# Three branch gates ahead of the mixers' end, halved block transposes and a later second low-rank visit in a hybrid transformer block

## The chip, the cores and the metric

The kernel runs on one core of a Trainium2 chip. TensorE (PE in the profile) multiplies matrices, VectorE (DVE) does elementwise arithmetic and 32x32 block transposes, ScalarE (ACT) does activations and rounding copies, GpSimd (POOL) does a few small operations, and SyncE (SP) issues the weight transfers. The metric is the device time in microseconds of one execution; lower is better. Times given as a median are over repeated runs; a profile shows one execution.

## The reference

One layer works on 256 tokens of 2048 features in fp32:

```
u = RMSNorm_pre(x)
proj = u @ w_in            # attention A (q,k,v), attention B (q,k,v,f), RWKV inputs, three gates
y_A = stick-breaking attention, y_B = forgetting attention, y_C = RWKV-7 time mixing (16 heads x 64)
m = sigmoid(g_a)*(y_A @ w_branch_a) + sigmoid(g_b)*(y_B @ w_branch_b) + sigmoid(g_c)*(y_C @ w_branch_c)
x = x + RMSNorm_post(m @ w_out)
x = x + RMSNorm_post2(relu(RMSNorm_pre2(x) @ w_up)^2 @ w_down)
```

The change lies where y_C is finished and where the third term of m, the one with g_c, begins.

## The kernel before, in words

**Weights.** All weights lie in DRAM as one stream of tiles of 128x1024 fp32 (512 KB), `wst`. `wraw` (L159) issues the next tile's DMA on SP's queue into one of three buffers `raw`; `wsplit` (L169) has ACT round it into `whi` (L172) and DVE subtract that from the tile to give `wlo` (L174). A product in fp32 is then made of three matmuls in the fp32r type: high by high, high by low, low by high. `wnext` (L177) keeps one tile ahead. The order of the tiles is that of the stream, except where the table `jump` (L153) gives another successor. `gc` is the first tile of the third branch. From there the stream holds, for each of four column groups g, eight tiles of gate weights (`gc + 12*g` on) and four tiles of `w_branch_c` (`gc + 12*g + 8` on). So in this kernel the order is: gate 0, gate 1, branch 0, branch 1, gate 2, branch 2, gate 3, branch 3.

**Products.** `unit` (L199) makes 128 output columns out of two tiles. `tok` (L207) makes 512 output columns for both halves of the tokens: for all tiles but the last it issues 12 matmuls (L234) and after that the last tile's 12 in two groups of six (`prod`, L219), one for each half of the tokens. So a gate, with eight tiles, is 84 matmuls of L234 and 12 of L219; a branch, with four tiles, is 36 and 12. `gate` (L999) runs `tok` on the normed input and has ACT write tanh into tiles `th` (L1003); its tiles have either their own tag or the tag `BK`, whose eight buffers the time mixing uses as well. `branch` (L1007) runs `tok` on the mixers' output and has DVE multiply by the gate (L1014) and add into `m` (L1015).

**Two strands of work.** PE's program order is that of the Python code. The products are one strand. The other is a generator, `mixers` (L943): attention A, attention B, the low-rank inputs of RWKV, and then `rwkv_half` (L665) for heads 0-7 and for heads 8-15. The products call `tick` (L137) a few times for each tile (in `tok` 0.7, 0.5 and 0.5, in `unit` 1.0 and 1.0). Each tick adds 0.62 times its argument to `credit` (at most 1.5) and takes its argument from `hold`; when `hold` is not positive and `credit` is, the generator is resumed. What it yields is the step's cost, taken from `credit`; a yield of `("stage", cost, h)` ends the resuming for this tick and sets `hold` to h (2.0 without h). So a pause h delays the generator by h worth of ticks. Order on the other engines is left to the compiler's scheduler; each engine then runs its own instructions in order.

**rwkv_half, in order.** The squares of k and the inverse norms; then for each of four pairs of heads its visit. A visit begins, for the first two pairs, with `gates` (L716) for two pairs at a time, whose low-rank matmuls (L723) take two of the four PSUM buffers `mps`; the visit itself (L771 to L790) takes four `mps` buffers for score blocks (L775), a transpose and a head sum, and DVE (L784, L789) and ACT (L787) read them out. At its end stands L790, `yield ("stage", 1.6)`. After the four visits 32x32 blocks are transposed on DVE into `U` (L814), a triangular system is solved in 31 steps (L819, L821), and the result is transposed back by DVE into `TW` (L825) and `SC` (L829). A scan over four chunks follows (L853 to L905, its last matmuls on `Bt` in L885), and then the group norm and output gate of the half, two pairs of heads at a time (L907 to L941): head sums on PE (L100, L101), gate products (L926, L929), an inverse root on ACT and DVE (`rsqrt`, L262 to L269) and products on DVE (L936 to L939).

**The third branch.** `cut` (L1025) splits each finished pair of heads of y_C into a high and a low part (L255 on ACT, L256 on DVE). L1033 runs two gates, with `cut` called at each tick; L1034 then resumes the generator until it ends, without any tick between; after that the branches run, the last tile of each in need of heads 12 to 15:

```
    thc = [gate(), gate("BK", 8)]
    while not fin[0]:
        step()
    cut()
```

Of the kernel before, what the change touches and what calls it, by code (L numbers as in the profile page):

```python
# [52 lines left out]
def hybrid_block(ctx, tc, xt, x, gains, params, consts, lora, gup, wst, out):  # L53
    nc = tc.nc
    V, A, G, PE = nc.vector, nc.scalar, nc.gpsimd, nc.tensor
# [10 lines left out]
    def nm(s):  # L66
        uid[0] += 1
        return f"{s}_{uid[0]}"
# [4 lines left out]
    def mps():  # L73
        return pm.tile([128, 512], F32, tag="mps", name=nm("mps"), bufs=4)
# [4 lines left out]
    def tmp(n=T):  # L79
        return tpool.tile([128, T], F32, tag="tmp", name=nm("tmp"), bufs=3)  # L80
# [5 lines left out]
    def C(name, r=slice(0, 128), lo=0, hi=None):  # L86
        c0, w = CC[name]
        hi = w if hi is None else hi
        if name == "ident":
            return ident[r, lo:hi]  # L90
        if c0 < NR + 128:
            return cr[r, c0 - 128 + lo:c0 - 128 + hi].bitcast(F32)
        return con[r, c0 - 128 - NR + lo:c0 - 128 - NR + hi]

    def CR(name):
        c0 = CC[name][0] - 128
        return cr[:, c0:c0 + 128]

    def twice(o, w, hi, lo):
        PE.matmul(o, w, hi, start=True, stop=False)  # L100
        PE.matmul(o, w, lo, start=False, stop=True)  # L101
# [48 lines left out]


    gc = wst.shape[0] - 256 - 32 - 48
    jump = {23: 28, 53: 24, 27: 54, gc + 7: gc + 12, gc + 19: gc + 8, gc + 11: gc + 20}  # L153
    wq = []
    side = []

# [50 lines left out]
    def tok(pks, lag=1, mid=()):  # L207


        ps = [gps(), gps()]  # L210
        n = len(pks)
        kept = []

        def prod(hl, k0, tt):
            for w, parts in ((hl[0], (0, T)), (hl[1], (0,))):
                for k in (k0, k0 + 1):
                    for part in parts:
                        c = part + tt * 128
                        PE.matmul(ps[tt], pks[k][:, c:c + 128], w[:, (k - k0) * 512:(k - k0) * 512 + 512],  # L219
                                  start=k == 0 and part == 0 and w is hl[0], stop=w is hl[1] and k == n - 1)  # L220

        for k0 in range(0, n, 2):
            hl = wnext()
            if k0 >= n - 2 * lag:
                prod(hl, k0, 0)
                kept.append((hl, k0))
                tick()
                continue
            for w, parts in ((hl[0], (0, T)), (hl[1], (0,))):
                for k in (k0, k0 + 1):  # L230
                    for tt in range(2):
                        for part in parts:
                            c = part + tt * 128
                            PE.matmul(ps[tt], pks[k][:, c:c + 128], w[:, (k - k0) * 512:(k - k0) * 512 + 512],  # L234
                                      start=k == 0 and part == 0 and w is hl[0], stop=False)
                    if w is hl[1] or k == k0:
                        tick(0.7 if w is hl[0] else 0.5)
        yield ps[0]
        for i, (hl, k0) in enumerate(kept):
            prod(hl, k0, 1)  # L240
            tick()
            if i < len(mid):
                mid[i]()
        yield ps[1]
# [31 lines left out]
    def g1(w=T):  # L276
        return rp.tile([128, T], F32, tag="g1", name=nm("g1"), bufs=21)
# [387 lines left out]
    def rwkv_half(hf):  # L665
# [12 lines left out]
        for i2 in range(2):  # L678
            hi, lo = pair(), pair()
            for i, p in enumerate(PR[2 * i2:2 * i2 + 2]):  # L680
                yield ("need", f"k{p}")
                kx[p] = done[f"k{p}"]
                s = tmp()
# [27 lines left out]
        SC = rp.tile([128, 32, 128], F32, tag="SC", name=nm("SC"), bufs=1)  # L711
# [52 lines left out]
        for i, p in enumerate(PR):  # L764
            for j in ((0, 1), (2, 3), (), ())[i]:
                yield from gates(j, PR[j])
            yield ("need", f"v{p}")
            yield ("stage", 0.4, 2.5 if i == 0 else 0)
            v, kp = done[f"v{p}"], kps[p]

            pss = [mps(), mps()]  # L771
            for cc in range(4):
                for h in range(2):
                    hr = slice(64 * h, 64 * h + 64)
                    PE.matmul(pss[h][:, cc * 128:cc * 128 + 128], At[p][hr, cc, :], Bt[p][hr, cc, :],  # L775
                              start=True, stop=True)
            psk = mps()
            for cc in range(4):
                PE.transpose(psk[:, cc * 128:cc * 128 + 128], At[p][:, cc, :], C("ident"))
            psb = mps()  # L780
            twice(psb[:, 0:T], CR("bones"), kp[:, 0, :], kp[:, 1, :])
            for h in range(2):
                s0 = i * 8 + h * 4
                V.tensor_tensor(SC[:, s0:s0 + 4, :], pss[h].rearrange("p (c t) -> p c t", c=4),  # L784
                                C("scm").unsqueeze(1).to_broadcast([128, 4, 128]), ALU.mult)
            Kt[p] = rp.tile([128, 4, 128], F32, tag="BK", name=nm("Kt"), bufs=8)
            A.activation(Kt[p], psk.rearrange("p (c t) -> p c t", c=4), AF.Copy)  # L787
            bon[p] = g1()
            V.tensor_tensor(bon[p], psb[:, 0:T], v, ALU.mult)  # L789
            yield ("stage", 1.6)  # L790

        pss = [mps(), mps()]
        for i, p in enumerate(PR):
# [12 lines left out]
        U = rp.tile([64, 32, 32], F32, tag="b6", name=nm("U"), bufs=1)  # L806
        Ti = rp.tile([64, 32, 32], F32, tag="Ti", name=nm("Ti"), bufs=1)
# [3 lines left out]
        G.memset(Tf[:, 0:1024:33], 1.0)  # L811
        for b in range(2):
            br = slice(32 * b, 32 * b + 32)
            V.transpose(out=U[br], in_=SC[br, :, 32 * b:32 * b + 32].rearrange("s l t -> s t l"))  # L814
            yield 1.3
        for s in range(31):
            n, m = 31 - s, s + 1
            t3 = tp[:, 0:n * m].rearrange("p (a b) -> p a b", a=n)
# [3 lines left out]
            yield 0.15 + n * m * 2.1e-3  # L822
        TW = rp.tile([64, 32, 32], F32, tag="b6", name=nm("TW"), bufs=1)

        V.transpose(out=TW[0:32].rearrange("t l i -> t i l"), in_=Ti[0:32].rearrange("l t i -> l i t"))  # L825
        yield 1.3
        for b in range(2):
            br = slice(32 * b, 32 * b + 32)
            V.transpose(out=SC[br, :, 32 * b:32 * b + 32].rearrange("i l t -> i t l"), in_=Ti[br])  # L829
            yield ("stage", 1.3, 1 + 3 * b)  # L830

        ps = mps()
        for j in range(32):
# [109 lines left out]
    def mixers():  # L943
        yield from sb_mix()
        yield from fox_mix()
        yield from rwkv_lora()
        for hf in range(2):
            yield from rwkv_half(hf)
# [15 lines left out]
    for br in ("sb", "fox"):  # L964
        for s in ("q", "k"):
# [3 lines left out]
            for h in range(4):  # L969
                ps = unit(upk)  # L970
                t = g1()
# [27 lines left out]
    def gate(tag="th", bufs=3):  # L999
        ths = []  # L1000
        for ps in tok(upk):
            th = rp.tile([128, 512], F32, tag=tag, name=nm("th"), bufs=bufs)
            A.activation(th, ps, AF.Tanh, scale=0.5)  # L1003
            ths.append(th)
        return ths
# [24 lines left out]

    cut()
    each.append(cut)
    thc = [gate(), gate("BK", 8)]  # L1033
    while not fin[0]:  # L1034
        step()
    cut()
# [52 lines left out]
    for c in range(0, D, 512):  # L1089
        for tt in range(2):  # L1090
            loads.append(lambda tt=tt, c=c: nc.sync.dma_start(out=x1[tt][:, c:c + 512],
                                                              in_=x[tt * 128:tt * 128 + 128, c:c + 512]))
# [410 lines left out]
    for g in range(4):  # L1503
        gs = slice(512 * g, 512 * g + 512)
        for tt, ps in enumerate(tok(hp, 4 if g == 3 else 1)):
# [8 lines left out]
            if g == 3:  # L1514
                for c, w in (0, 512), (512, 512), (1024, 512), (1536, 256), (1792, 256):
# [3 lines left out]
                        out=out[tt * 128:tt * 128 + 128, cs], in_=x1[tt][:, cs])  # L1519
# [125 lines left out]
```

## Time and profile before

| | us |
|---|---|
| median of three runs | 1519.75 (1519.08 to 1521.86) |
| the profiled execution | 1519.93 |
| its span, first to last instruction | 1518.2 |
| PE busy | 1495.3 (98%) |
| weight loads on PE busy | 1254.8 (83%) |
| DVE busy | 1208.3 (80%) |
| ACT busy | 939.7 (62%) |
| POOL busy | 99.6 (7%) |

The 1.7 us between the execution and its span lie outside the first and last instruction. The profile numbers time from the span's start. The attention and RWKV inputs, the mixers and the three branches fill about the first 830 us; the output projection and the MLP fill the rest. A row of a timeline gives start, duration, engine, line, operation, output and inputs, shape and count; in brackets stands how long the engine was idle before and what released it. A row of the chain gives start, duration, engine, output and line of a piece of work on the path that ends last.

### The profile page before, as it was taken

The numbers are of one execution on the slowest core, as the hardware profiler recorded it, in microseconds if no ns is written. First come the engines' busy times: TensorE is split into PE (matmuls) and PEld (weight loads), VectorE is DVE, ScalarE is ACT, GpSimd is POOL, SyncE is SP. The second block draws the span as 40 slices with busy tenths as digits, with TensorE's granted clock in tenths as the row PEclk, the third lists the DMA queues.
The fourth block names the chain that finished last, engine by engine and source line by source line (L and its number), as shares of the span: only waits on it lengthen the run. The fifth ranks groups of instructions, "written<-read, shape, count | busy, mean of one in ns | idle before, by whom it ended". The sixth has DMA issues, their size and how long they took to land.

```text
span 1518.2 us, 22692 instructions
## 1 busy us (share of the span) xinstructions
PE 1495.3 (98%) x8384; PEld 1254.8 (83%) x8384; DVE 1208.3 (80%) x1663; ACT 939.7 (62%) x1433; POOL 99.6 (7%) x151
## 2 busy tenths in 40 slices
PE   9999999999999999989999999999999999999997
PEld 7888888887787877778888988888888888888886
DVE  7875669985678885565656778999899989999996
ACT  7665677545776445644445766677666666766663
POOL 0031003000002000000000000000000000000000
PEclk9999999999999999999999999999999999999999
DMA  7645454454455464445575758879888888889874
GB/s 266 194 167 181 148 172 156 157 190 144 157 170 181 145 195 147 156 152 194 203 249 189 242 173 263 235 226 275 247 256 265 242 249 245 263 263 259 253 221 151
DMA packets 104687, 312.71 MB, mean 206 GB/s; under 512 B 10240, under 2 KB 12288, under 8 KB 104576
## 3 DMA queue, kind: packets, MB, share of 16 engines
q1 hardware_dynamic: 93968, 279.87, 55.2%
q0 software_dynamic: 8064, 29.36, 10.1%
q10 hardware_dynamic: 2544, 2.03, 0.5%
q8 instruction: 66, 1.08, 0.3%
q14 instruction: 45, 0.37, 0.1%
HBM read 279.77 MB, written 2.10 MB: 186 GB/s over the span
## 4 chain that ended last, share of the span: by engine, by line
PE 86%; DVE 6%; DMA 3%; issue 2%; ACT 2%; DVEq 0%; POOLq 0%; SPq 0%; POOL 0%; ACTq 0%
PE gps L234 25%; PE gps L190 19%; PE gps L194 11%; PE gps L219 7%; PE mps L1363 3%; PE mps L1365 3%; PE mps L1364 3%; PE gps L1363 2%; PE gps L1365 2%; PE gps L1364 2%; DMA raw<-in_wst_dram 2%; DVE wlo L174 2%; PE gps L196 1%; ACT whi L172 1%; DMA raw<-raw 1%
## 5 line engine op out<-in xcount | busy, mean ns | idle before, releaser
L174 DVE TENSOR_TENSOR wlo<-raw,whi 128x1024 fp32r<-128x1024 f32 x576 | 697.7, 1221 | 176.0 <-ACT whi L172 158.5
L172 ACT ACTIVATE whi<-raw 128x1024 fp32r<-128x1024 f32 x576 | 603.9, 1056 | 257.1 <-PE gps L234 91.7
L190 PE MATMUL gps<-pk,whi 128*128 128x512 f32 x1479 | 375.7, 392 | 1.8 <-DVE tmp L1281 1.6
L190 PEld LDWEIGHTS gps<-pk,whi 128*128 128x128 f32 x1479 | 273.9, 188 | 57.7 <-DVE tmp L1281 2.6
L234 PE MATMUL gps<-whi,pk 128*128 128x512 f32 x1004 | 254.6, 392 | 0.0
L194 PEld LDWEIGHTS gps<-pk,wlo 128*128 128x128 f32 x1582 | 215.5, 190 | 15.7 <-DVE wlo L174 0.8
L194 PE MATMUL gps<-pk,wlo 128*128 128x256 f32 x1582 | 221.1, 282 | 0.0
L234 PEld LDWEIGHTS gps<-whi,pk 128*128 128x128 f32 x1004 | 186.4, 188 | 39.7 <-issue 0.8
L234 PE MATMUL gps<-wlo,pk 128*128 128x512 f32 x502 | 137.7, 392 | 1.1 <-DVE wlo L174 1.1
L234 PEld LDWEIGHTS gps<-wlo,pk 128*128 128x128 f32 x502 | 93.2, 188 | 21.9 <-DVE wlo L174 2.0
L1363 PE MATMUL mps<-whi,fm 128*128 128x512 f32 x224 | 88.6, 396 | 0.8 <-ACT whi L172 0.5
L1364 PE MATMUL mps<-whi,fm 128*128 128x512 f32 x224 | 87.7, 392 | 0.0
L1280 ACT ACTIVATE tmp<-gps 128x256 f32<-128x256 f32 x64 | 24.6, 384 | 101.7 <-PE gps L196 99.8
L1365 PE MATMUL mps<-wlo,fm 128*128 128x512 f32 x224 | 87.4, 390 | 0.0
L1343 POOL DMA_DIRECT2D raw<-raw x56 | 48.8, 872 | 573.2 <-DVE raw L1340 279.8
L1340 DVE TENSOR_TENSOR raw<-raw,raw 128x1024 f32<-128x1024 f32 x56 | 68.3, 1220 | 0.8
L219 PE MATMUL gps<-whi,pk 128*128 128x512 f32 x224 | 63.0, 404 | 4.6 <-ACT pk L255 4.6
L1363 PE MATMUL gps<-whi,fm 128*128 128x512 f32 x168 | 65.8, 392 | 0.0
L1365 PE MATMUL gps<-wlo,fm 128*128 128x512 f32 x168 | 65.8, 392 | 0.0
L1364 PE MATMUL gps<-whi,fm 128*128 128x512 f32 x168 | 65.5, 390 | 0.0
L219 PEld LDWEIGHTS gps<-whi,pk 128*128 128x128 f32 x224 | 42.3, 193 | 14.4 <-ACT pk L255 5.0
L1365 PEld LDWEIGHTS mps<-wlo,fm 128*128 128x128 f32 x224 | 42.1, 188 | 9.6 <-DVE wlo L174 0.2
(346 smaller groups left out, 1732.2 us busy)
## 6 DMA issues: line engine op xcount, KB each, us to landing
raw<-in_wst_dram SPq DMA_DIRECT2D x516, 512.0 KB, 4.4
raw<-raw POOLq DMA_DIRECT2D x56, 512.0 KB, 8.2
x<-in_xt_dram SPq DMA_DIRECT2D x8, 256.0 KB, 6.8
x<-in_x_dram SPq DMA_DIRECT2D x8, 256.0 KB, 5.0
raw<-in_wst_dram SPq DMA_DIRECT2D x4, 256.0 KB, 4.8
g<-in_gains_dram SPq DMA_DIRECT2D x4, 256.0 KB, 4.9
pk<-in_gains_dram SPq DMA_DIRECT2D x4, 256.0 KB, 7.4
out_dram<-x SPq DMA_DIRECT2D x4, 256.0 KB, 2.8
```

Source lines behind the costliest of these rows:

```text
L172: A.activation(hi, raw, AF.Copy)
L174: low = lambda: V.tensor_tensor(lo, raw, hi.bitcast(F32), ALU.subtract)
L190: PE.matmul(ps, hi[:, i * 128:i * 128 + 128], pks[i], start=first and i == 0, stop=False)
L194: PE.matmul(ps[:, 0:T], lo[:, i * 128:i * 128 + 128], pks[i][:, 0:T], start=False, stop=False)
L219: PE.matmul(ps[tt], pks[k][:, c:c + 128], w[:, (k - k0) * 512:(k - k0) * 512 + 512], start=k == 0 and part == 0 and w is hl[0], stop=w is ...
L234: PE.matmul(ps[tt], pks[k][:, c:c + 128], w[:, (k - k0) * 512:(k - k0) * 512 + 512], start=k == 0 and part == 0 and w is hl[0], stop=False)
L1280: A.activation(b, ps[:, T:2 * T], AF.Copy)
L1340: V.tensor_tensor(R[d, a], R[d, a], R[d, b], ALU.add)
L1343: G.dma_start(out=R[d, a], in_=R[d, b], accum_op=ALU.add)
L1363: PE.matmul(Q[f], a, w, start=d == d0 and i == 0, stop=False)
L1364: PE.matmul(Q[f], b, w, start=False, stop=False)
L1365: PE.matmul(Q[f], a, wl, start=False, stop=d == dn and i == 1)
```

## The change

There are four edits.

1. A third gate, for column group 2, is run at L1033 before the generator is driven to its end, with its two output tiles in `BK` buffers.
2. `jump` is rewritten so that the weight tiles come in the new order: gate 0, gate 1, gate 2, branch 0, branch 1, branch 2, gate 3, branch 3.
3. The pause after the visit of the first pair (L790) becomes 3.5 ticks in place of the default 2.0; other pairs keep 2.0.
4. Each of the five block transposes of a half (two of L814, one of L825, two of L829) is made in two instructions of half the columns. Each half has a step cost of 0.65 in place of 1.3 for the whole; the pauses at L830 become 0.5, 0.5, 0.5 and 3.5 in place of 1 and 4.

```diff
-    jump = {23: 28, 53: 24, 27: 54, gc + 7: gc + 12, gc + 19: gc + 8, gc + 11: gc + 20}
+    jump = {23: 28, 53: 24, 27: 54, gc + 7: gc + 12, gc + 19: gc + 24, gc + 31: gc + 8,
+            gc + 11: gc + 20, gc + 23: gc + 32}
...
-            yield ("stage", 1.6)
+            yield ("stage", 1.6, 3.5 if i == 0 else 2.0)
...
-            V.transpose(out=U[br], in_=SC[br, :, 32 * b:32 * b + 32].rearrange("s l t -> s t l"))
-            yield 1.3
+            for c in (slice(0, 16), slice(16, 32)):
+                V.transpose(out=U[br, c], in_=SC[br, :, 32 * b:32 * b + 32][:, :, c].rearrange("s l t -> s t l"))
+                yield 0.65
...
-        V.transpose(out=TW[0:32].rearrange("t l i -> t i l"), in_=Ti[0:32].rearrange("l t i -> l i t"))
-        yield 1.3
+        for c in (slice(0, 16), slice(16, 32)):
+            V.transpose(out=TW[0:32, :, c].rearrange("t l i -> t i l"), in_=Ti[0:32, :, c].rearrange("l t i -> l i t"))
+            yield 0.65
...
-            V.transpose(out=SC[br, :, 32 * b:32 * b + 32].rearrange("i l t -> i t l"), in_=Ti[br])
-            yield ("stage", 1.3, 1 + 3 * b)
+            for c in (slice(0, 16), slice(16, 32)):
+                V.transpose(out=SC[br, :, 32 * b:32 * b + 32][:, :, c].rearrange("i l t -> i t l"), in_=Ti[br, c])
+                yield ("stage", 0.65, 0.5 + 3 * b * (c.start > 0))
...
-    thc = [gate(), gate("BK", 8)]
+    thc = [gate(), gate("BK", 8), gate("BK", 8)]
```

## The prediction, made before the result was known

> **What bounds the kernel now.** The first thing to read is the busy time on the page.
>
> ```profile
> PE 1495.3 (98%) x8384; PEld 1254.8 (83%) x8384; DVE 1208.3 (80%) x1663; ACT 939.7 (62%) x1433; POOL 99.6 (7%) x151
> ```
>
> PE is busy for 98% of the span, and the change takes no matmul away. All that it can win is time in which PE waits or runs slowly. So the second view is that of the waits, for PE alone, over the stretch of the mixers, 220 to 660 us (in total, how often, the longest):
>
> ```profile
> PE gps L219 <- ACT pk L255: 4.6, 1, 4.6
> PE gps L234 <- DVE wlo L174: 1.1, 2, 0.9
> PE gps L219 <- DVE wlo L174: 1.0, 2, 0.6
> PE mps L723 <- DVE SC L784: 0.9, 1, 0.9
> ```
>
> That is everything: 7.6 us in six waits, of which one alone is 4.6. The same view from 662.65 to 860 us names no wait of PE. The chain of waits, third, shows what the long one is:
>
> ```profile
> 642.65 0.23 PE mps L100
> ...
> 657.13 0.42 ACT pk L255
> 657.55 0.04 issue
> 657.60 5.22 PE gps L219 x12
> 662.82 8.16 PE gps L234 x36
> 670.98 2.72 PE gps L219 x12
> 673.70 19.04 PE gps L234 x84
> 692.74 2.72 PE gps L219 x12
> ```
>
> Gate 1 ends at 642.65. The head sums of the last two pairs (L100) come right behind it, and from there a serial tail runs over ACT and DVE: two table loads with the logarithm and exponential, the inverse root, the products, the split (L255). It ends at about 657.6, after 15 us. Beside it PE has only the first three tiles of branch 0 (about 8.2 us by the row of 36 matmuls); the fourth needs the last heads. The 12 matmuls of that fourth tile take 5.22 us where all their like take 2.72. The stretches show why (busy us and count of PE, weight loads, DVE, ACT, POOL, then the granted clock, the DMA's share and GB/s):
>
> ```profile
> 653.00:657.60 4.60, 0.00 (x1) 0.00 (x1) 4.38 (x11) 1.74 (x5) 0.00 (x0) 0.77 0.65 218
> 657.60:660.00 2.40, 2.40 (x6) 1.86 (x7) 0.74 (x2) 0.28 (x1) 0.00 (x0) 0.50 0.45 176
> 660.00:662.65 2.65, 2.65 (x8) 2.12 (x7) 1.38 (x2) 0.30 (x1) 0.00 (x0) 0.56 0.02 6
> 662.65:665.40 2.75, 2.75 (x14) 2.27 (x13) 2.43 (x3) 1.45 (x2) 0.00 (x0) 1.00 0.00 0
> ```
>
> The granted clock falls during the wait and stays at 0.50 to 0.56 until 662.65. So the wait costs 4.6 us and then 5.22 - 2.72 = 2.5 us more, 7.1 in all.
>
> **The third gate.** It puts eight tiles of work that need no mixer between gate 1's end and branch 0: 84 and 12 matmuls, 19.04 + 2.72 = 21.8 us by the last rows of the chain. Does the tail fit under it? By the code, after the head sums the generator still yields 0.1 + 2.2 + 1.1 + 1.1 = 4.5 of cost. A tile of a gate gives 1.7 ticks, 1.05 of credit, so these steps take 4.3 tiles. The pause before the head sums (2.5 ticks) adds at most 1.5 tiles. Edit 3 delays each half by at most a tile of a gate (seven ticks in place of four), less what credit is kept over the pause. At worst the generator ends after 4.3 + 1.5 + 2 = 7.8 of 8 tiles. Behind its last step stand at most some 4.6 us of DVE and ACT (the stretch from 653.00 to 657.60 has all of it, DVE 4.38 busy), and branch 0's fourth tile comes another 8.2 us after the gate. There is room even then. I take the whole **7.1 us** as gained; the bounds are 7.1 and, if the tail still ends last, 0 (below, as a rival).
>
> What the gate brings with it is moved and not new: eight transfers, eight roundings on ACT, eight subtractions on DVE, two tanh. In SP's queue the eight loads go ahead of branches 0 and 1; from 600 to 720 us that queue holds nothing else, and POOL's holds nothing:
>
> ```profile
> raw<-in_wst_dram SPq DMA_DIRECT2D x37, 512.0 KB, 3.2
> ```
>
> The new tanh tiles need two more BK buffers. The last reader of Bt there starts before 620 us, some 40 us before the third gate's first tanh could write, so ACT waits for no buffer:
>
> ```profile
> L885 PE MATMUL mps<-Bt,Pb x96: 222/222/270, 361.6 to 618.7; 128*64 128x64 f32 x96
> ```
>
> Three branches now follow one another where two did. A branch has 8.16 + 2.72 = 10.9 us of PE; DVE's share is four subtractions of 1.2 us and four products and sums of 0.69 (the rows of L174 and L1014 below), 7.6 us. That hides, and two in a row showed no PE wait.
>
> **The pause.** The wait of L723 is for PSUM: its two buffers come free when L784 has read the first pair's scores.
>
> ```profile
> 247.76 0.98 PE L723 MATMUL mps<-xs,lors 64*128 64x256 f32 x12 [0.88 <-DVE SC L784]
> 248.23 0.40 DVE L789 TENSOR_TENSOR g<-mps,g 128x256 f32<-128x256 f32 x1
> ```
>
> In this half the ticks are 1.0, so 3.5 means two ticks or one tile more (about 2.7 us). By then L784 and L789 have ended, and the wait goes: **0.9 us**, bounds 0 and 0.9. The other half's L723 shows no wait and only gets later. Behind the delayed visit stand all later steps of the generator; they end at most two tiles later, which the third gate covers as worked out above. Without that gate it would lengthen the 4.6 us.
>
> **The transposes.** Price of one, and what a short DVE instruction costs (ns least/median/most in the first row):
>
> ```profile
> L814 DVE STREAM_TRANSPOSE U<-SC x4: 2003/2016/2027, 276.7 to 504.1; 32x1024 f32<-32x1024 f32 x4
> ```
> ```profile
> 507.28 0.19 DVE L819 TENSOR_TENSOR tp<-U,Ti 64x31 f32<-64x31 f32 x1
> ...
> 522.36 0.42 DVE L819 TENSOR_TENSOR tp<-U,Ti 64x256 f32<-64x256 f32 x1
> ```
>
> From 31 to 256 elements 0.23 us are added, about 1.0 ns an element, which leaves 0.16 us that doesn't scale. The trace shows no half transpose. If it shrinks with its elements it takes 1.0 us, or 1.1 with 0.16 fixed; if it doesn't shrink at all, 2.0. I take 1.1, the row of the same engine, so ten more instructions add 1.6 us of DVE in two halves. [...]
>
> What the halves give: a subtraction can pass between them. Two of PE's waits lie at transposes:
>
> ```profile
> 329.68 2.06 DVE L829 STREAM_TRANSPOSE SC<-Ti 32x1024 f32<-32x1024 f32 x1
> ...
> 333.44 1.20 PE L234 MATMUL gps<-wlo,pk 128*128 128x512 f32 x4 [0.91 <-DVE wlo L174]
> ```
> ```profile
> 549.00 1.06 ACT L172 ACTIVATE whi<-raw 128x1024 fp32r<-128x1024 f32 x1 [0.92 <-DMA raw<-in_wst_dram]
> ...
> 550.94 0.72 PE L219 MATMUL gps<-wlo,pk 128*128 128x512 f32 x2 [0.56 <-DVE wlo L174]
> ```
>
> The first I believe: the subtraction stood behind this whole transpose and the one before it. The second has a late transfer ahead of it, which only in part goes back to DVE. Bounds 0 and 0.9 + 0.6 = 1.5; I take **0.7**, near the middle.
>
> **New small waits.** Steps of the mixers now meet other tiles. The waits for wlo that lie at no transpose sum to 1.1 + 1.0 - 1.5 = 0.6 us now. They may go (0.6 gained) or as much as all 2.1 us of waits for wlo may come anew. I take 0.6 lost.
>
> **Sum.** 7.1 + 0.9 + 0.7 - 0.6 = 8.1 us. The profiled execution took 1519.93, which gives 1511.8; it lies 0.18 above the median of the runs, so in terms of that median **1511.6 us**. The likeliest case's own range: all gains at their best (7.1 + 0.9 + 1.5 + 0.6 = 10.1) give 1509.6; the gate's gain alone less 2.1 gives 1514.7.
>
> **The rivals.**
>
> *A wait remains under the new gate.* The tail now competes with eight tiles' roundings and subtractions where it had four, and PE waits for some wlo, or for the last split, again. For it: from 642 to 653 us ACT was nearly full (9.2 of 11 us). Against: PE waited for nothing in these 11 us, with the same tail beside it.
>
> ```profile
> 500.00:553.00 53.00, 52.44 (x261) 43.03 (x258) 51.21 (x91) 24.23 (x32) 0.00 (x0) 1.00 0.48 159
> 642.00:653.00 11.00, 10.98 (x49) 8.30 (x47) 6.08 (x8) 9.16 (x11) 0.00 (x0) 1.00 0.38 118
> ```
>
> Price: from where the likeliest range ends to half of the 7.1 and a little, 1514.7 to 1516.7. Chance 0.08. Waits up to 0.9 us left the clock at 1.00 in this trace and the one of 4.6 did not. [...]
>
> *The change doesn't do what it says.* The generator, slowed by two pauses, still ends last, behind the gate, and the wait with its clock comes back whole: 1511.6 + 7.1 = 1518.7, within 0.2% of before. It needs the tail to be over 12 us later than worked out. Chance 0.04.
>
> *Slower: half a transpose costs as much as a whole.* Then each half of the heads gets five more instructions of 2.0 us, 10 us. Place: the stretch from 500 to 553 us and its like in the first half of the heads. DVE is busy there for 51.2 of 53 us, so only 1.8 us hide; the other 8.2 us push the subtractions back and PE with them, twice: 16.4 us, 1528.0. It decides from 1.8 us for a half transpose on, where two times (5 x 0.8) us eat the 8.1. Against it: DVE's other rows shrink with their elements, L819 above, and L1014 with half of L174's elements takes 0.69 to its 1.22 us:
>
> ```profile
> L174 DVE TENSOR_TENSOR wlo<-raw,whi 128x1024 fp32r<-128x1024 f32 x6 | 7.3, 1220 | 4.2 <-ACT whi L172 4.2
> ...
> L1014 DVE SCALAR_TENSOR_TENSOR th<-th,gps 128x512 f32<-128x512 f32 x2 | 1.4, 689 | 3.1 <-PE gps L219 3.1
> ```
>
> Chance 0.06.
>
> **How the numbers follow.** The forecast has 0.82, the rivals 0.08, 0.04 and 0.06. A measurement of this kernel can tell about 0.2% (3.0 us) from no change, so faster means under 1516.7. That holds for the forecast's range and the first rival: 0.82 + 0.08, from which I give 0.03 to "same" since the first rival's end lies on that line. Faster 0.87, same 0.07, slower 0.06. The range goes from 1509.5 to 1516.0: the forecast's own and most of the first rival, leaving the second and third out.
>
> **What would show it.** Right: no wait of PE over 1 us between 600 and 700 us, a granted clock of 1.00 there, the branch's six-matmul groups all near 1.36 us; L723 without a wait in the first half; half transposes near 1.1 us; no wait at the first half's L829. Wrong: a wait on L255 or on wlo in the third gate, half transposes near 2 us, or new waits on wlo between 250 and 600 us that sum to more than 2 us.

## The result and the profile after

The changed kernel took **1511.3 us** (median of eight runs, 1509.64 to 1513.97); the kernel before took 1519.3 in eight runs beside them (1516.52 to 1521.86). The ratio is 0.9953, with a 95% interval of 0.9944 to 0.9962: 5.8 to 8.5 us faster. The profiled execution of the changed kernel took 1513.32 us, 2 us above its median, with a span of 1511.5. Code lines in its profile are one to four higher than before.

First the waits of PE over the mixers, 220 to 660 us, in total, how often and the longest:

```profile
PE gps L235 <- DVE wlo L175: 1.9, 1, 1.9
PE mps L845 <- ACT TW L841: 0.7, 4, 0.2
```

The wait of 4.6 us is gone, and so are the one at the low-rank matmuls (L723 before) and all the old waits for wlo. Two kinds that were not there before stand in their place: one wait of 1.9 us for wlo, and four of up to 0.2 us each at L845. The chain of work around gate 1's end, with start and duration:

```profile
642.38 2.72 PE gps L220 x12
645.10 4.99 PE gps L235 x22
650.08 0.23 PE mps L100
...
652.04 14.28 PE gps L235 x62
666.32 2.72 PE gps L220 x12
669.03 8.16 PE gps L235 x36
677.20 2.72 PE gps L220 x12
```

Only PE stands in it now. The head sums come 5 us into the third gate, the tail runs beside the rest of the gate, and the fourth tile of branch 0 (677.20) takes 2.72 us. The granted clock is 1.00 from 640 to 675 us. The last split, from the timeline:

```profile
663.48 0.75 DVE L257 TENSOR_TENSOR pk<-g,pk 128x256 fp32r<-128x256 f32 x2
```

It ends at 664.2, 13 us before the tile that needs it. But gate 1 ends at 645.10, where it ended at 642.65 before: up to here the changed kernel is 2.4 us behind, with the same work done (4095 instructions of PE in both). Further on it is ahead. The first transpose of the MLP's input, on PE, before and after (the duration in ns, then first and last start in us):

```profile
L1125 PE MATMUL mps<-ident,x x32: 270/272/328, 827.0 to 837.8; 128*128 128x128 f32 x32
```
```profile
L1129 PE MATMUL mps<-ident,x x32: 270/272/328, 822.3 to 833.1; 128*128 128x128 f32 x32
```

It starts 4.7 us earlier, so 2.4 + 4.7 = 7.1 us were won between gate 1's end and 827 us. The last 2.0 us of the 6.7 by which the spans differ come in the MLP, which the change doesn't touch: the profile before has 1.6 us of waits on evictions there (L190) that this one lacks. That part is not steady from one execution to the next. In the thirteen profiles of this case, from the row above to the end of the span, it takes between 688.7 and 691.2 us.

Where the 2.4 us went shows in stretches (busy us and counts of PE, weight loads, DVE, ACT and POOL, then the granted clock, DMA's share and GB/s):

```profile
344.00:346.50 2.50, 1.81 (x66) 1.22 (x66) 1.23 (x1) 2.39 (x5) 0.00 (x0) 1.00 0.48 164
346.50:350.50 4.00, 4.00 (x12) 3.08 (x11) 1.22 (x1) 2.31 (x7) 0.00 (x0) 0.57 0.71 245
468.30:469.60 1.30, 1.30 (x6) 0.85 (x8) 1.30 (x2) 0.42 (x1) 0.00 (x0) 1.00 0.31 63
469.60:473.20 3.60, 3.60 (x24) 3.28 (x25) 2.59 (x5) 1.54 (x2) 0.00 (x0) 0.53 0.88 286
```

Behind each of the two places with new waits lies a stretch of about 3.4 us at a granted clock of 0.50 (the 0.57 and 0.53 above are means that take in its edges), where PE has work. The 12 matmuls of branch 0's last tile took 5.22 us at 0.50 to 0.56 in the kernel before and take 2.72 at 1.00 here; if the work in these stretches also takes about half as long at 1.00, each can cost up to 1.7 us, which is an estimate. New waits of 1.9 + 0.7 and old ones of 0.9 + 2.1 gone leave 0.4 us won, so to be 2.4 us behind, the two stretches must have cost 2.4 + 0.4 = 2.8 us in this one execution. That is a difference, not a measurement of its own, and it fits under the 3.4 us that two such stretches can cost.

### The profile page after: what moved, and what is told of

Same layout as the page of the kernel before. It is cut to its first block, busy times and chain, and to the rows that moved or that the text cites. A ratio compares the mean times of both kernels' runs of the same rounds, so it can differ in the third digit from the quotient of the medians.

```text
span 1511.5 us, 22706 instructions
## 1 busy us (share of the span) xinstructions
PE 1494.9 (99%) x8384; PEld 1256.2 (83%) x8384; DVE 1208.5 (80%) x1673; ACT 938.9 (62%) x1433; POOL 99.5 (7%) x151
## 3 DMA queue, kind: packets, MB, share of 16 engines
q8 instruction: 66, 1.08, 0.3%
## 4 chain that ended last, share of the span: by engine, by line
PE 90%; DVE 4%; DMA 3%; issue 2%; ACT 1%; DVEq 0%; POOLq 0%; SPq 0%; POOL 0%; ACTq 0%
PE gps L235 26%; PE gps L191 21%; PE gps L195 11%; PE gps L220 7%; PE mps L1367 3%; PE mps L1369 3%; PE mps L1368 3%; PE gps L1369 2%; PE gps L1367 2%; PE gps L1368 2%; DMA raw<-in_wst_dram 2%; PE gps L197 1%; DVE wlo L175 1%; DMA raw<-raw 1%; PE mps L776 1%
## 5 line engine op out<-in xcount | busy, mean ns | idle before, releaser
L235 PEld LDWEIGHTS gps<-whi,pk 128*128 128x128 f32 x1004 | 187.0, 188 | 40.1 <-issue 0.8
L1367 PEld LDWEIGHTS mps<-whi,fm 128*128 128x128 f32 x224 | 42.3, 189 | 9.1 <-ACT whi L173 3.0
```

Source lines behind the costliest of these rows:

```text
L1367: PE.matmul(Q[f], a, w, start=d == d0 and i == 0, stop=False)
```

## The experiments

Each kernel is timed against the kernel before on the same chip. The medians of before in the four sets were 1518.44, 1518.1, 1518.33 and 1518.86 us.

### Each edit by itself

**The third gate alone** (edits 1 and 2; the lines of `jump` are those of the change):

```diff
...
-    thc = [gate(), gate("BK", 8)]
+    thc = [gate(), gate("BK", 8), gate("BK", 8)]
```

> The third gate and its tile order alone, pause and transposes as before. My account (the wait of 4.6 us and 2.5 us at half clock both go, because 21.8 us of gate cover the tail): 7.1 us faster, some 1512.3 by the first median, no wait of PE near 650 us, granted clock 1.00 there, and the waits at L723 (0.9) and on wlo (2.1) still there. Rival (the gate gives only the wait, and the rest of the measured 8 us comes from pause and transposes): 4.6 us faster, some 1515.

Measured: 1511.62 us, ratio 0.9960 (0.9948 to 0.9972), so 4.3 to 7.9 us faster; the medians lie 6.8 apart. Its chain:

```profile
639.97 2.72 PE gps L220 x12
642.69 0.23 PE mps L100
...
644.65 19.27 PE gps L235 x84
663.91 2.72 PE gps L220 x12
666.63 8.16 PE gps L235 x36
674.79 2.72 PE gps L220 x12
```

Until gate 1's end nothing has moved (642.69 to 642.65), and its small waits up to there are those of the kernel before. The fourth tile of branch 0 takes 2.72 us, the time of its like in the kernel before at a granted clock of 1.00. The 7.1 us lie within the interval and so do 4.6. The trace decides: from the same gate 1's end, the first transpose of the MLP's input (L1126 here) starts at 819.9 us where it started at 827.0, so 7.1 us are gone and not 4.6.

**The pause alone** (edit 3):

```diff
-            yield ("stage", 1.6)
+            yield ("stage", 1.6, 3.5 if i == 0 else 2.0)
```

> The longer pause alone, with two gates. My account: the 0.9 us wait of L723 goes, but the generator is up to two tiles later at gate 1's end, so more of the tail lies behind it and the wait before branch 0's last tile grows from 4.6 us by 0 to 5 us: same to 4 us slower. Rival (the pause is free, its delay is made up by kept credit): 0.9 us faster, wait unchanged at 4.6.

Measured: 1520.82 us, ratio 1.0013 (1.0005 to 1.0022), 0.8 to 3.3 us slower. Its waits from 220 to 665 us:

```profile
PE mps L100 <- ACT hl L919: 3.2, 1, 3.2
PE gps L234 <- DVE wlo L174: 2.6, 3, 1.9
PE gps L219 <- DVE pk L256: 0.8, 1, 0.8
PE gps L219 <- ACT pk L255: 0.5, 1, 0.5
PE mps L101 <- DVE hl L920: 0.2, 1, 0.2
```

The wait of L723 is gone. In the place of the 4.6 us stand 3.2 + 0.2 at the head sums and 1.3 behind: about as much, but earlier, since the later tail doesn't have its head sums' inputs ready when gate 1 ends. And a wait of 1.9 us for wlo is new. So the pause isn't free, and the delay shows where I expected it, in another form. But all these waits sum to 7.3 us, where those of before sum to 7.6, so they are not what makes the kernel slower. Behind the 1.9 us, the next 34 matmuls of PE take 6.5 us (465.73 to 472.26), where the same 34 take 4.9 with gate and pause (465.85 to 470.80), at a clock of 1.00: 1.6 us more, or by estimate some 3.2 us at half clock. Behind the 3.2 us lie some 6.8 us of it:

```profile
647.00:650.00 3.00, 2.77 (x10) 1.51 (x9) 1.50 (x2) 2.60 (x4) 0.00 (x0) 0.67 0.07 26
650.00:655.00 5.00, 5.00 (x13) 3.73 (x12) 1.39 (x2) 3.30 (x4) 0.00 (x0) 0.51 0.23 89
```

PE has work in nearly all of it. In the kernel before, the slow clock (0.50) also lasts some 6.8 us, but it begins about 2 us before the wait ends, while PE has nothing to do. The cost of the pause alone is that of the clock more than that of waits.

**The halved transposes alone** (edit 4; its diff is that of the change):

> The halved transposes alone, with two gates. By the prediction: half transposes of 1.1 us, the 0.9 us wait at the first half's L829 gone, 0.7 us faster, the 4.6 us wait unchanged. Rival (small waits only move to other tiles and clock drops come with them): within 1 us of before, waits on wlo that sum to about 2 us in other places.

Measured: 1518.42 us, ratio 1.0003 (0.9994 to 1.0012): no difference that can be told. Its waits from 220 to 660 us, beside the two of 4.6 and 0.9 that are as before:

```profile
PE gps L234 <- DVE wlo L174: 0.8, 2, 0.6
PE gps L219 <- DVE wlo L174: 0.5, 1, 0.5
PE mps L844 <- ACT TW L840: 0.2, 1, 0.2
```

The waits for wlo fall from 2.1 to 1.3, and 0.2 are new: 0.6 us, close to the 0.7 of the prediction. The interval of the time is 2.7 us wide and can't show that.

### The edits in pairs

**Pause and transposes, two gates:**

> Both of the smaller edits without the third gate. The profile of the changed kernel shows them 2.5 us behind by gate 1's end. If they cost that in most runs (new waits of 1.9 and 0.7 us and two stretches at half clock), this kernel is 2 to 7 us slower than before, since the later tail also lengthens the wait of 4.6 us. If that profile was an unlucky one and the edits give what was predicted, it is within 2 us of before.

Measured: 1519.56 us, ratio 1.0012 (1.0003 to 1.0021), 0.5 to 3.2 us slower. The lower part of that belongs to the second account, the upper to the first, so neither is out; a cost of 4 us or more is. The profile has the 1.9 and the 3.2 us of waits of the pause alone: the cost is the pause's, as it is without the transposes.

**Third gate and pause; third gate and transposes:**

> The third gate with the longer pause, transposes whole. If the pause gives its 0.9 us under the gate's cover: 8.0 us faster than before, 0.9 better than the gate alone. If new waits elsewhere eat it: 6 to 7 us faster, like the gate alone or worse.

> The third gate with halved transposes, pause as before. If the halves give 0.7 us or more: 7.8 us faster than before. If small waits only move: 6 to 7 us faster, and the profile shows waits on wlo or TW elsewhere.

Measured: 1512.14 us, ratio 0.9956 (0.9944 to 0.9969), and 1510.71 us, ratio 0.9953 (0.9941 to 0.9966). Beside 0.9960 for the gate alone and 0.9953 for all of it, no pair can be told from the gate alone by time. The cost that the pause has without the gate can't be seen under it, but the intervals leave room for it.

The traces separate what the times can't. The first low-rank matmul (L723 before) starts before all that the edits touch, and the first transpose of the MLP's input after it. Between the two lie, in one execution each:

| kernel | us between | less than before |
|---|---|---|
| before | 604.5 | |
| third gate | 597.4 | 7.1 |
| pause | 607.2 | -2.7 |
| transposes | 603.8 | 0.7 |
| pause and transposes | 605.0 | -0.5 |
| third gate and pause | 596.7 | 7.8 |
| third gate and transposes | 596.4 | 8.1 |
| the changed kernel | 599.8 | 4.7 |

The halved transposes give 0.7 us without the gate and 1.0 with it. The pause gives 0.7 under the gate in the one profile in which the granted clock stays at 1.00 at its new wait; the changed kernel, with two slow stretches, is 2.4 us worse than the gate alone. What the pause is worth hangs on whether the clock falls there.

### Does the wait cost more than itself?

**Filling the wait:** in the kernel before, ahead of branch 0's last tile:

```diff
...
             if k0 >= n - 2 * lag:
+                if filler:
+                    idle = mps()
+                    for _ in range(filler.pop()):
+                        PE.matmul(idle, upk[0][:, 0:128], upk[0], start=True, stop=True)
                 prod(hl, k0, 0)
...
+        if g == 0:
+            filler.append(16)
```

> The kernel before with 16 matmuls of 128x512 whose result nobody reads, put ahead of branch 0's last tile, so that PE runs them (about 3.5 us) during the wait for the last heads. Nothing useful is moved and the wait for the heads stays. My account (the wait drops the clock, and the slow clock costs 2.5 us behind it): granted clock 1.00 through this place, the 12 matmuls of L219 take 2.7 us and not 5.2, 2.5 us faster than before. Rival (those 12 are slow because their inputs, the split heads, come piece by piece): still about 5 us for them, no change in time.

Measured: 1517.35 us, ratio 0.9994 (0.9985 to 1.0003), from 2.3 us faster to 0.5 slower. The stretches, and the 12 matmuls of branch 0's last tile:

```profile
653.00:657.60 4.60, 3.64 (x17) 2.67 (x15) 4.39 (x10) 1.74 (x5) 0.00 (x0) 1.00 0.70 224
657.60:660.80 3.20, 3.17 (x13) 2.40 (x14) 1.95 (x4) 0.57 (x2) 0.00 (x0) 1.00 0.41 145
```
```profile
657.63 1.44 PE L220 MATMUL gps<-whi,pk 128*128 128x512 f32 x4 [0.99 <-ACT pk L260]
...
659.38 1.08 PE L220 MATMUL gps<-whi,pk 128*128 128x512 f32 x4
...
660.30 0.62 PE L220 MATMUL gps<-wlo,pk 128*128 128x512 f32 x2
```

With matmuls in the wait the clock stays at 1.00, though a wait of 1.0 us is left behind them. The last tile starts where it did (657.63 to 657.60) and is done at 660.92, where it took until 662.82 before: 1.9 us earlier. So the slow tile is the clock's doing, for 1.9 us. Of the rest of my 2.5, some 0.6 us (3.3 to 2.72) is left in the filled kernel too and so is not the clock's; the larger part lies in the first four matmuls (1.44 us to the 1.08 of the next four), which go as the split comes piece by piece. By the time alone the matter would be open: 1.9 lies in the interval, and so does 0. But the first transpose of the MLP's input starts 1.9 us earlier as well (825.1 to 827.0).

### Where the new wait of 1.9 us comes from

Both kernels below have the third gate and the halved transposes, and the long pause in one half of the heads alone; the third is the changed kernel on the same chip.

```diff
-            yield ("stage", 1.6, 3.5 if i == 0 else 2.0)
+            yield ("stage", 1.6, 3.5 if i == 0 and hf == 0 else 2.0)
```

That is the pause in the first half; for the second it reads `hf == 1`.

> The changed kernel with the longer pause in the first half of the heads alone. If the wait of 1.9 us near 468 us comes from the pause in the second half and the 0.9 us wait of L723 goes by the pause in the first: neither of the two in the profile, about 1 us faster than gate and transposes without a pause (1509.7), and 1.9 us or more faster than the changed kernel on this chip. If the wait near 468 us is not the pause's: it is still there, and the time is that of the changed kernel.

> The changed kernel with the longer pause in the second half of the heads alone. By the same account: both the 0.9 us wait of L723 and the 1.9 us wait near 468 us are there, so it is 1 us slower than the changed kernel and the slowest of the three sent together. Otherwise the wait of 1.9 us is gone.

> The changed kernel itself, on the same chip as the two variants of its pause: 0.9953 of before, with the 1.9 us wait near 468 us. [...]

Measured: 1512.6 us, ratio 0.9958 (0.9944 to 0.9971); 1511.06 us, ratio 0.9953 (0.9941 to 0.9966); 1511.79 us, ratio 0.9957 (0.9945 to 0.9970). The times don't separate them, but the waits do. First all waits with the pause in the first half, then the longest one with the pause in the second:

```profile
PE gps L235 <- DVE wlo L175: 1.9, 1, 1.9
PE mps L845 <- ACT TW L841: 0.8, 5, 0.2
```
```profile
PE mps L724 <- DVE SC L785: 0.9, 1, 0.9
```

My account was wrong. The wait near 468 us comes from the pause in the **first** half, some 220 us earlier; with the pause in the second half alone it isn't there. The timeline shows how. First the gate alone, without a pause, then gate and pause, at the same place:

```profile
460.95 0.68 DVE L1015 SCALAR_TENSOR_TENSOR th<-th,gps 128x512 f32<-128x512 f32 x1
...
461.55 1.22 DVE L175 TENSOR_TENSOR wlo<-raw,whi 128x1024 fp32r<-128x1024 f32 x1
...
462.68 0.69 DVE L1016 TENSOR_TENSOR m<-m,th 128x512 f32<-128x512 f32 x1
```
```profile
459.50 1.05 ACT L173 ACTIVATE whi<-raw 128x1024 fp32r<-128x1024 f32 x1
...
460.50 0.92 DVE L754 TENSOR_TENSOR At<-g,em 128x256 f32<-128x256 f32 x1
...
461.34 0.91 DVE L752 SCALAR_TENSOR_TENSOR At<-kkr,tha 128x256 f32<-128x256 f32 x1
...
462.18 1.27 DVE L1015 SCALAR_TENSOR_TENSOR th<-th,gps 128x512 f32<-128x512 f32 x2
463.37 1.28 DVE L1016 TENSOR_TENSOR m<-m,th 128x512 f32<-128x512 f32 x2
...
464.58 1.22 DVE L175 TENSOR_TENSOR wlo<-raw,whi 128x1024 fp32r<-128x1024 f32 x1
...
465.85 1.20 PE L235 MATMUL gps<-wlo,pk 128*128 128x512 f32 x4 [1.87 <-DVE wlo L175]
```

Without the pause the subtraction passes between the products and sums of a branch. With it the second half's low-rank steps (L747, L754, L752) come just ahead of that branch's end on DVE, then its four operations in a row (2.5 us), and only then the subtraction for which PE waits. Its inputs had long been there: counted from the start of the kernel it is subtraction 143, and rounding 143 is the row at 459.50, done at 460.55, four microseconds before the subtraction starts at 464.58. DVE is busy all that time. So it is DVE's order that makes the wait, and no late transfer.

**A pause that is one tick longer**, in the first half alone, with gate and transposes:

```diff
-            yield ("stage", 1.6, 3.5 if i == 0 else 2.0)
+            yield ("stage", 1.6, 2.75 if i == 0 and hf == 0 else 2.0)
```

> The changed kernel with a pause of 2.75 (one tick, half a tile, longer than before) in the first half of the heads alone, 2.0 in the second. If the wait of 1.9 us near 468 us is a matter of which tile the second half's steps meet, a shift of half a tile can miss it: L723 without its 0.9 us wait, no wait of 1.9 us, waits between 220 and 660 us that sum to about 1.3 us, the best of all versions at some 1509.8. If the steps of the second half snap to the same tile as with a whole tile's shift, the 1.9 us are there again and the time is that of the changed kernel.

Measured: 1510.6 us, ratio 0.9945 (0.9932 to 0.9959), the lowest of all, though its interval overlaps that of the changed kernel. Its waits from 220 to 660 us are all of these:

```profile
PE gps L235 <- DVE wlo L175: 1.2, 3, 0.6
PE gps L220 <- DVE wlo L175: 0.5, 1, 0.5
PE mps L845 <- ACT TW L841: 0.2, 1, 0.2
```

The wait of L723 is gone and that of 1.9 us didn't come: half a tile's shift misses the place that a whole tile's shift meets. The sum is 1.9 us, not the 1.3 expected. Between the two rows of the table above lie 596.5 us, as with gate and transposes and no longer pause (596.4), so that pause gains nothing that shows.

## Why the prediction was right, and where it wasn't

- **The time**, 1511.6 foretold and 1511.3 measured, is right, and so is what carries it. The gate's 7.1 us are what the pair of traces shows between gate 1's end and 827 us; the trace of the gate alone shows the same 7.1, and its time 4.3 to 7.9. The tail fits with more room than worked out: 13 us before branch 0's fourth tile, where the worst case left about 4. That the medians agree to 0.3 us is luck: the interval is 2.7 us wide, and of the 8.1 us foretold the 1.0 of the smaller edits is not shown.
- **The clock's share of the wait**, 2.5 us, had the right mechanism and was somewhat too large: 1.9 us go when the wait is filled, about 0.6 stay. With the gate both go.
- **The pause**, 0.9 us gained: the wait of L723 goes, as foretold. The step that failed is that the later steps would only end later, under the gate's cover. That holds for the end of the generator (the pause alone costs 0.8 to 3.3 us, under the gate nothing that the time can tell), but its delay also moves the second half's steps to other tiles, where PE waits 1.9 us and the clock can fall behind that (to 0.50 for 3.4 us in both profiles of the changed kernel). With the gate alone it takes away other waits and is 0.7 us ahead in a profile without the slow clock; with gate and halved transposes it is behind in all three profiles that have that wait, by 1.9 to 3.4 us (598.2, 598.9 and 599.8 us to 596.4 between the two rows of the table).
- **The transposes**: a half takes 1.06 to 1.14 us, against 1.1. In the changed kernel, by line and shape (total busy, mean ns, idle before):

```profile
L833 DVE STREAM_TRANSPOSE SC<-Ti 32x512 f32<-32x512 f32 x8 | 8.7, 1091 | 0.1
...
L828 DVE STREAM_TRANSPOSE TW<-Ti 32x512 f32<-32x512 f32 x4 | 4.4, 1144 | 0.1
```

  The slower rival, that a half costs as much as a whole, is out. (Its limit, 1.8 us for a half, was worked out too high: by the same paragraph's terms, five halves more and 1.8 us hidden in each half of the heads, 8.1 us are eaten from about 1.6 us on. At 1.1 measured nothing hangs on it.) The gain of 0.7 us is 0.6 in the waits, 0.7 and 1.0 in the traces, and too small for the time to show.
- **The new small waits**, 0.6 us, were undersized: 1.9 + 0.7 us, and in the profiled execution 2.8 us lost at half clock, which had no term in the sum. The prediction named new waits for wlo of more than 2 us as a sign of being wrong; they came to 1.9, just under it. In that execution the smaller edits lost 2.4 us together, where the prediction gave them 1.0 (0.9 + 0.7 - 0.6) gained. The medians, 8.0 us apart with 7.1 of them the gate's, leave room for a small gain instead. Whether these edits gain or lose in the median stays open.
- **The first rival**, a wait that remains under the gate, didn't come: PE waits for nothing between 640 and 860 us.

## What to carry to other kernels

Look behind a long wait of TensorE, not only at it: here the work behind a wait of 4.6 us ran at a clock of 0.50 to 0.56, and independent work put into the wait won both, 7.1 us. When work is interleaved by counted pauses, a pause shifts every later meeting of the two strands; a small wait cured at one place can come back, larger, further on (here 0.9 us went and 1.9 us came some 220 us later), so read the waits of the whole stretch and not only of the place. Try the smaller edits apart from the large one: here the third gate, with its tile order, gave all that the time can show. Where the total is too unsteady to tell, measure in the traces between two instructions that lie around the edits.

## What the runs showed of the hardware

Behind a wait of 1.9 us, far shorter than 4.6 us, the clock fell too, and not in every profile. Six profiles have that wait. In both of the changed kernel a stretch of 3.4 us at half clock follows. In the pause alone and in the pause in the first half the matmuls behind it are slow as well: 1.87 us for the 16 of L775 and 1.44 us for the first ten of L776, where gate with pause has 1.16 us for all 16, at 1.00 throughout. For pause with transposes the mean granted clock of the span is 0.996 and for the pause alone 0.995, which leaves it open there. The changed kernel in its second profile, and gate with pause:

```profile
468.30:472.00 3.70, 3.70 (x22) 3.24 (x19) 2.58 (x4) 1.54 (x2) 0.00 (x0) 0.54 0.89 309
```
```profile
465.80:470.00 4.20, 4.15 (x32) 3.36 (x33) 3.39 (x5) 1.08 (x2) 0.00 (x0) 1.00 0.65 207
```

In the first profile of the changed kernel a stretch near 345 us with only 0.7 us of waits in four pieces, among small 32x32 matmuls, was followed by 3.4 us at half clock too (the row from 346.50 us above); its second profile has 0.5 us of such waits in three pieces, and its span is 1.6 us shorter (1509.9 to 1511.5 us). Why the same wait costs the clock in one profile and not in another, and how long a wait must be for that, no run here shows. Over the changed kernel's eight runs the mean granted clock goes from 0.996 to 0.999: the shortest span, 1507.9 us, has 0.999, and the three longest, 1511.5 to 1512.2, have 0.996 and 0.997. The version with the one-tick pause had 0.998 in all six of its runs, and its times spread over 2.6 us.
